# Six weight buffers at six offsets past multiples of 512 bytes, and a smaller scratch for dynamic DMAs

## The chip, the cores and the metric

The kernel runs on one core of one Trainium2 chip. Five engines with queues of their own share the core's SBUF, a memory of 128 partitions: TensorE (PE in the rows; its weight loads stand apart as PEld), VectorE (DVE), ScalarE (ACT), GpSimd (POOL) and SyncE (SP, which issues most DMAs). The metric is device microseconds of one execution. The kernel before takes 622.99 us, the median of 2 runs (622.51 to 623.47).

## The reference

One decoder layer on x of 512 rows and 1024 columns, all in float32:

```python
xn = rms_norm(h, g_mix_norm[l])
proj = xn @ w_in[l]                                  # 1024 x 2560: q, k, v, and u for the convolution
attn = moba_attention(q, k, to_heads(v))             # 8 heads of 64, blocks of 256
conv = conformer_conv(u, b_glu[l], w_dw[l], b_dw[l], g_conv_ln[l], b_conv_ln[l])   # GLU, 31 taps, LayerNorm, swish
h = h + jnp.concatenate([attn, conv], axis=-1) @ w_out[l]
ff = jnp.square(jax.nn.relu(rms_norm(h, g_mlp_norm[l]) @ w_mlp_in[l]))             # 1024 x 4096
h = h + ff @ w_mlp_out[l]                            # 4096 x 1024
return rms_norm(h, g_final)
```

## The kernel before, in words

Every large product is made of float32 values that are split in two: a high part, which is the value rounded to the type fp32r, and a low part, the rest. A product is then three matmuls: high by high, high by low and low by high. `mm3` (L155 to L161) issues the three one after the other into one PSUM bank, on lines L158, L159 and L160. Each of these matmuls loads its own stationary operand first, 128 rows by 128 columns (a LDWEIGHTS in the rows), and then streams a moving operand of 512 or 256 columns past it. A stationary tile is 512 bytes in a partition, a moving one 2048 or 1024.

The weights are cut into 92 units of 128 by 1024 values. For each unit SP loads `raw` (4 buffers), ACT makes the high part `wh` (L115), and DVE, at a few places POOL, makes the low part `wl` (L116). There are three buffers for `wh` and three for `wl`, used in turn: these are the six weight buffers. Four of the units, those of the second half of w_out, go to other buffers (`ffhw`, `fflw`, L126 and L127).

The stages, in order of time:

- u (to about 60 us): the convolution's inputs. The stationary operand is a piece of `wh` or `wl`, the moving one is x, transposed and split (`xh`, `xl`).
- q, k, v, attention and convolution (60 to 227 us): the moving operand of q, k and v is `wh` or `wl`, the stationary one `xh` or `xl`. DVE and POOL run the 31 taps of the convolution here (L300, L323). A table of places (`T`) sets the order of the attention's steps.
- y (200 to 263 us): the output projection, then the second norm and transposes into `hTh`, `hTl`.
- MLP (263 to 611 us): four chunks. In each, `ff` (8 blocks) has the stationary operand in `wh` or `wl` and the moving one in `hTh` or `hTl`; then `z` (two halves) has the moving operand in `wh` or `wl` and the stationary one in `ffh` or `ffl`.
- The last norm and the stores.

Where the buffers lie: in the kernel before all six weight buffers begin at a multiple of 4096 bytes, and so do `xh`, `xl` (later `mixh`, `mixl`), `hTh`, `hTl`, `ffh` and `ffl`. The last four are in the pool `pm`, which takes the place of the attention's pool `pa`; a tile `shift` that nothing uses (L689) sets where `pm` begins. A piece of 128 columns is 512 bytes, so that every stationary and every moving operand of the stages u, q, k, v, y, ff and z begins at a multiple of 512 bytes.

The only DMAs that POOL issues are two on L422, which copy `qs` from one half of the partitions to the other. The scratch for dynamic DMAs is 16 KB at the beginning of SBUF.

Of the kernel before, what the change touches and what calls it, by code (L numbers as in the profile page):

```python
# [10 lines left out]
F32 = mybir.dt.float32  # L11
FR = mybir.dt.float32r
# [5 lines left out]
P = 128  # L18
# [36 lines left out]
def hybrid_layer(ctx: ExitStack, tc: tile.TileContext, x, pack, w_in, w_out, g_mlp, w1, w2, g_fin, out):  # L55
    nc = tc.nc

    perm = ctx.enter_context(tc.tile_pool(name="perm", bufs=1))
# [9 lines left out]
    def f32(ap):  # L68
        return ap.bitcast(F32)
# [23 lines left out]
    raws, parts = {}, {}  # L93
    RAW, SPL = 4, 3

    def load_unit(pieces=1, between=None):
        n = len(raws)
        if n < len(srcs):
            raw = perm.tile([P, 1024], F32, tag="raw", name=f"raw{n}", bufs=RAW)
            a = srcs[n].shape[1]  # L100
            for i in range(pieces):
                r = slice(i * a // pieces, (i + 1) * a // pieces)
                nc.sync.dma_start(raw.rearrange("p (a b) -> p a b", a=a)[:, r], srcs[n][:, r])
                if between and i < pieces - 1:
                    between()
            raws[n] = raw

    def split_unit(pieces=1, low=nc.vector, between=None):
        n = len(parts)
        if n < len(srcs):  # L110
            hi = perm.tile([P, 1024], FR, tag="wh", name=f"wh{n}", bufs=SPL)
            lo = perm.tile([P, 1024], FR, tag="wl", name=f"wl{n}", bufs=SPL)
            for i in range(pieces):
                c = slice(i * 1024 // pieces, (i + 1) * 1024 // pieces)
                nc.scalar.copy(hi[:, c], raws[n][:, c])  # L115
                low.tensor_tensor(lo[:, c], raws[n][:, c], f32(hi[:, c]), op=OP.subtract)  # L116
                if between:
                    between(i)
            a = srcs[n].shape[1]
            parts[n] = (hi.rearrange("p (a b) -> p a b", a=a), lo.rearrange("p (a b) -> p a b", a=a))  # L120
            load_unit()

    def resident_unit(hi, lo):
        n = len(parts)
        raw = raws[n].rearrange("p (a b) -> p a b", a=srcs[n].shape[1])
        nc.scalar.copy(hi, raw)  # L126
        eng(f"er{n % 4}").tensor_tensor(lo, raw, f32(hi), op=OP.subtract)  # L127
        parts[n] = None
        nunit[0] += 1
        load_unit()  # L130
# [3 lines left out]
    def unit(ahead=2):  # L134
        n = nunit[0]
        nunit[0] += 1
        while len(parts) < min(n + 1 + ahead, len(srcs)):
            split_unit()
        return parts[n]
# [39 lines left out]
    nc.sync.dma_start(pk, pack)  # L179
    load_x(1, slice(0, 512))  # L180
    load_unit(2, load_rest)
    load_unit(2)
    load_unit()
# [94 lines left out]
    transpose_half(0, tx)  # L278
    store_half(0, tx, range(0, 4))
    split_unit(4, low=nc.gpsimd, between=lambda i: i and store_half(0, tx, range(2 * i + 2, min(2 * i + 4, KD))))  # L280
    split_unit(4)
    split_unit()
    for t in range(NT):
# [402 lines left out]
    phA.close()  # L686
    pm = ctx.enter_context(tc.tile_pool(name="pm", bufs=1, reuse_waits="tile"))

    pm.tile([P, 928], F32, name="shift")  # L689
    gml = perm.tile([P, D], F32, tag="gbc", name="gmlpbc", bufs=1)  # L690
    nc.scalar.dma_start(gml, bass.AP(tensor=g_mlp.tensor, offset=g_mlp.offset, ap=[[0, P], [1, D]]))

# [207 lines left out]
```

## Time and profile before

| | |
|---|---|
| Median of 2 runs | 622.99 us |
| The profiled execution | 623.05 us, of which the trace spans 621.3 us |
| PE busy | 578.2 us (93% of the span) |
| DVE, ACT, POOL busy | 369.7, 266.1, 162.9 us |
| Mean granted clock of TensorE | 0.968 |
| Mean share of the DMA traffic | 92 GB/s |

A row of a timeline has a start, a duration, the engine, the line, the operation and out<-in. Matmuls overlap in the pipeline, so that the duration of one is longer than what it adds; what a matmul adds is the distance from its start to the next one's, and it is read from two rows and the number of matmuls between them. A row of --lines kind has a count after the x, then busy time, the mean of one in ns, and the idle time before. In rows by windows each engine has its busy time and, in brackets, its number of instructions; then come the granted clock, the DMA share and GB/s.

### The profile page before, as it was taken

How to read it: one execution, taken by the hardware profiler on the slowest of the kernel's cores; microseconds unless marked ns; L12 is line 12 of the kernel's file. 1: busy time of each engine (PE TensorE's matmuls, PEld its weight loads, DVE VectorE, ACT ScalarE, POOL GpSimd, SP SyncE). 2: the span in 40 equal slices, each digit the busy share in tenths (PEclk: the TensorE clock that was granted, in tenths of full speed). 3: DMA queues.
4: the chain of work that ended last, by engine and by line, in shares of the span. 5: the costliest groups of instructions: out<-in, count | busy, mean ns of one | idle time of the engine just before them, and what ended most of it. 6: DMA issues, size and time to landing. Idle time of an engine off the chain costs nothing.

```text
span 621.3 us, 7312 instructions
## 1 busy us (share of the span) xinstructions
PE 578.2 (93%) x2768; PEld 476.7 (77%) x2768; DVE 369.7 (59%) x486; ACT 266.1 (43%) x445; POOL 162.9 (26%) x170
## 2 busy tenths in 40 slices
PE   8998692876999999999999999999999999999995
PEld 7986562765767788898888888888888888888884
DVE  4589999999989766746424454431455343345243
ACT  6864263663768773435321144322234222334233
POOL 2496598492887551100000000000000000000002
PEclk9999987896999999999999999999999999999998
DMA  8632122161111156205233322233232333222203
GB/s 265 153 98 66 38 68 67 35 135 34 56 47 35 35 205 169 69 1 170 101 102 101 93 78 102 102 102 101 72 99 101 103 101 102 86 86 99 69 0 137
DMA packets 59380, 57.22 MB, mean 92 GB/s; under 512 B 1872, under 2 KB 42960, under 8 KB 59344
## 3 DMA queue, kind: packets, MB, share of 16 engines
q1 hardware_dynamic: 58512, 54.64, 28.6%
q0 software_dynamic: 544, 1.05, 1.0%
q10 hardware_dynamic: 288, 1.05, 0.4%
q8 instruction: 22, 0.36, 0.2%
q14 instruction: 14, 0.11, 0.1%
HBM read 53.59 MB, written 2.10 MB: 90 GB/s over the span
## 4 chain that ended last, share of the span: by engine, by line
PE 76%; DVE 15%; issue 3%; ACT 2%; POOL 2%; DMA 1%; SPq 0%; POOLq 0%; ACTq 0%; DVEq 0%
DVE acc L300 10%; PE ff L159 9%; PE ff L158 9%; PE ff L160 9%; PE z L159 9%; PE z L158 9%; PE z L160 9%; DVE wl L116 3%; PE y L158 2%; PE y L160 2%; PE y L159 2%; PE u L160 1%; PE u L159 1%; PE u L158 1%; PE pt L497 1%
## 5 line engine op out<-in xcount | busy, mean ns | idle before, releaser
L116 DVE TENSOR_TENSOR wl<-raw,wh 128x1024 fp32r<-128x1024 f32 (+1 forms) x86 | 113.2, 1318 | 100.6 <-ACT wh L115 100.3
L115 ACT CAST wh<-raw 128x1024 fp32r<-128x1024 f32 (+1 forms) x94 | 92.6, 991 | 117.8 <-PE z L160 75.3
L323 POOL TENSOR_TENSOR acc<-acc,ct 128x512 f32<-128x512 f32 x60 | 98.2, 1636 | 23.2 <-ACT ct L313 19.5
L158 PE MATMUL ff<-hTh,wh 128*128 128x512 f32 (+1 forms) x280 | 103.9, 371 | 0.0
L159 PE MATMUL ff<-hTl,wh 128*128 128x512 f32 (+1 forms) x280 | 103.8, 371 | 0.0
L160 PE MATMUL ff<-hTh,wl 128*128 128x512 f32 (+1 forms) x280 | 103.8, 371 | 0.0
L159 PE MATMUL z<-wl,ffh 128*128 128x512 f32 (+1 forms) x264 | 101.0, 383 | 0.0
L158 PE MATMUL z<-wh,ffh 128*128 128x512 f32 (+1 forms) x264 | 101.0, 383 | 0.0
L160 PE MATMUL z<-wh,ffl 128*128 128x512 f32 (+1 forms) x264 | 101.0, 383 | 0.0
L699 POOL TENSOR_SCALAR ms0f<-ms_f 128x1 f32<-128x1 f32 x4 | 0.8, 192 | 328.7 <-ACT f L223 328.7
L300 DVE SCALAR_TENSOR_TENSOR acc<-hin,pk,acc 128x512 f32<-128x512 f32 x60 | 83.0, 1384 | 1.4
L763 DVE TENSOR_TENSOR sq<-rl 128x512 f32<-128x512 f32 x32 | 22.2, 692 | 64.3 <-ACT rl L761 64.3
L158 PEld LDWEIGHTS ff<-hTh,wh 128*128 128x128 f32 x280 | 52.8, 188 | 9.1
L160 PEld LDWEIGHTS ff<-hTh,wl 128*128 128x128 f32 x280 | 52.7, 188 | 9.0
L159 PEld LDWEIGHTS ff<-hTl,wh 128*128 128x128 f32 x280 | 52.8, 188 | 9.0
L158 PEld LDWEIGHTS z<-wh,ffh 128*128 128x128 f32 x264 | 49.6, 188 | 9.8
L160 PEld LDWEIGHTS z<-wh,ffl 128*128 128x128 f32 x264 | 49.6, 188 | 9.7
L159 PEld LDWEIGHTS z<-wl,ffh 128*128 128x128 f32 x264 | 49.6, 188 | 9.6
L761 ACT ACTIVATE rl<-ff 128x512 f32<-128x512 f32 x32 | 19.2, 599 | 82.6 <-PE ff L160 82.6
L313 ACT ACTIVATE ct<-hin,pk 128x512 f32<-128x512 f32 x60 | 41.5, 719 | 17.9 <-POOL acc L323 17.5
L765 DVE TENSOR_TENSOR ffl<-sq,ffh 128x512 fp32r<-128x512 f32 x32 | 22.2, 693 | 21.9 <-ACT ffh L764 21.9
L764 ACT CAST ffh<-sq 128x512 fp32r<-128x512 f32 x32 | 19.8, 620 | 25.5 <-DVE sq L763 25.5
(162 smaller groups left out, 899.5 us busy)
## 6 DMA issues: line engine op xcount, KB each, us to landing
raw<-w SPq DMA_DIRECT2D x64, 512.0 KB, 3.9
raw<-w_in SPq DMA_DIRECT2D x18, 512.0 KB, 3.7
raw<-w_out SPq DMA_DIRECT2D x8, 512.0 KB, 3.7
xr<-x SPq DMA_DIRECT2D x4, 512.0 KB, 5.0
out<-ot SPq DMA_DIRECT2D x8, 256.0 KB, 2.0
x<-x SPq DMA_DIRECT2D x4, 256.0 KB, 4.4
raw<-w_in SPq DMA_DIRECT2D x4, 256.0 KB, 5.9
x<-x SPq DMA_DIRECT2D x2, 512.0 KB, 6.9
```

Source lines behind the costliest of these rows:

```text
L115: nc.scalar.copy(hi[:, c], raws[n][:, c])
L116: low.tensor_tensor(lo[:, c], raws[n][:, c], f32(hi[:, c]), op=OP.subtract)
L158: nc.tensor.matmul(ps, sh, mh, start=first, stop=False)
L159: nc.tensor.matmul(ps, sh, ml, start=False, stop=False)
L160: nc.tensor.matmul(ps, sl, mh, start=False, stop=last)
L300: nc.vector.scalar_tensor_tensor(accs[i], hins[i][:, j:j + S], wtap(i, j), accs[i], op0=OP.mult, op1=OP.add)
L313: nc.scalar.activation(tmp, hins[i][:, j:j + S], AF.Copy, scale=wtap(i, j))
L323: nc.gpsimd.tensor_tensor(acc, acc, products[n], op=OP.add)
L761: nc.scalar.activation(rl, ps, AF.Relu)
L763: nc.vector.tensor_mul(sq, rl, rl)
L764: nc.scalar.copy(ff["h"][:, b], sq)
L765: nc.vector.tensor_sub(ff["l"][:, b], sq, f32(ff["h"][:, b]))
```

## The change

```diff
+    WH_AT, WL_AT = (16, 64, 8), (96, 32, 48)
...
     def split_unit(pieces=1, low=nc.vector, between=None):
         n = len(parts)
         if n < len(srcs):
-            hi = perm.tile([P, 1024], FR, tag="wh", name=f"wh{n}", bufs=SPL)
-            lo = perm.tile([P, 1024], FR, tag="wl", name=f"wl{n}", bufs=SPL)
+            b = n % SPL
+            hi = perm.tile([P, 1152], FR, tag=f"wh{b}", name=f"wh{n}", bufs=1)[:, WH_AT[b]:WH_AT[b] + 1024]
+            lo = perm.tile([P, 1152], FR, tag=f"wl{b}", name=f"wl{n}", bufs=1)[:, WL_AT[b]:WL_AT[b] + 1024]
...
-    pm.tile([P, 928], F32, name="shift")
+    pm.tile([P, 1184], F32, name="shift")
...
-    nc = bacc.Bacc("TRN2", target_bir_lowering=False, num_devices=1)
+    nc = bacc.Bacc("TRN2", target_bir_lowering=False, num_devices=1, dynamic_dma_scratch_size=8192)
```

Each weight buffer grows by 512 bytes, and the 1024 values begin at a different place in it: past a multiple of 512 bytes, the three `wh` begin at 0x40, 0x100 and 0x20, the three `wl` at 0x180, 0x80 and 0xC0. The scratch for dynamic DMAs falls from 16 KB to 8 KB, which makes the room. Tiles ahead of the weight buffers move down by 8192 bytes, those of `pa` by 5120, and those of `pm`, with the longer `shift`, by 4096: `xh`, `xl`, `hTh`, `hTl`, `ffh` and `ffl` still begin at multiples of 4096 bytes.

Nothing else changes. The built program has the same 4521 instructions in the same order on every engine, and every wait is for the same semaphore at the same value. What differs is the start of an operand in the weight buffers, in 2280 matmuls, in the 94 instructions that write a `wh` and in the 94 that read it and write a `wl` (the first two units are split in four pieces).

## Rows read from the trace of the kernel before

**Rows 1.** Page, part 1: busy time by engine.
```profile
PE 578.2 (93%) x2768; PEld 476.7 (77%) x2768; DVE 369.7 (59%) x486; ACT 266.1 (43%) x445; POOL 162.9 (26%) x170
```
**Rows 2.** Page, part 4: the chain that ended last, by engine, by line.
```profile
PE 76%; DVE 15%; issue 3%; ACT 2%; POOL 2%; DMA 1%; SPq 0%; POOLq 0%; ACTq 0%; DVEq 0%
DVE acc L300 10%; PE ff L159 9%; PE ff L158 9%; PE ff L160 9%; PE z L159 9%; PE z L158 9%; PE z L160 9%; DVE wl L116 3%; PE y L158 2%; PE y L160 2%; PE y L159 2%; PE u L160 1%; PE u L159 1%; PE u L158 1%; PE pt L497 1%
```
**Rows 3.** Busy time by windows: the convolution and attention, then the MLP.
```profile
60.00:227.00 167.00, 136.60 (x636) 104.52 (x634) 152.66 (x236) 102.70 (x201) 115.17 (x98) 0.90 0.22 67
263.00:611.00 348.00, 348.00 (x1622) 291.71 (x1621) 147.40 (x168) 107.82 (x145) 3.41 (x11) 1.00 0.29 90
```
**Rows 4.** Timeline of PE in z, first and last of 16 matmuls.
```profile
400.01 0.39 PE L160 MATMUL z<-wh,ffl 128*128 128x512 f32 x1
...
403.41 0.39 PE L160 MATMUL z<-wh,ffl 128*128 128x512 f32 x1
```
**Rows 5.** Timeline of PE in ff, first and last of 16 matmuls.
```profile
285.09 0.39 PE L160 MATMUL ff<-hTh,wl 128*128 128x512 f32 x1
...
288.49 0.39 PE L160 MATMUL ff<-hTh,wl 128*128 128x512 f32 x1
```
**Rows 6.** Timeline of PE in ff with 256 columns, first and last of 19.
```profile
264.03 0.28 PE L160 MATMUL ff<-hTh,wl 128*128 128x256 f32 x1
...
266.19 0.28 PE L160 MATMUL ff<-hTh,wl 128*128 128x256 f32 x1
```
**Rows 7.** Timeline of PE in q, first and last of six matmuls.
```profile
60.88 0.63 PE L160 MATMUL q<-wh,xl 128*128 128x512 f32 x1
...
63.01 0.47 PE L159 MATMUL q<-wl,xh 128*128 128x512 f32 x1
```
**Rows 8.** Windows around rows 7 and rows 4: the granted clock is third from last.
```profile
60.00:63.00 3.00, 3.00 (x8) 2.32 (x7) 2.93 (x3) 2.78 (x4) 2.84 (x3) 0.50 0.63 180
400.00:403.40 3.40, 3.40 (x16) 2.81 (x15) 0.88 (x1) 1.05 (x1) 0.00 (x0) 1.00 0.43 157
```
**Rows 9.** By line and shape: matmuls with an operand in a weight buffer.
```profile
L158 PE MATMUL z<-wh,ffh 128*128 128x512 f32 x248 | 96.5, 389 | 0.0
L158 PE MATMUL ff<-hTh,wh 128*128 128x512 f32 x232 | 90.3, 389 | 0.0
L158 PE MATMUL u<-xh,wh 128*128 128x512 f32 x40 | 15.6, 389 | 0.0
L158 PE MATMUL u<-xh,wh 128*128 128x256 f32 x48 | 13.8, 288 | 0.0
L158 PE MATMUL ff<-hTh,wh 128*128 128x256 f32 x48 | 13.7, 284 | 0.0
L158 PE MATMUL z<-wh,ffh 128*128 128x256 f32 x16 | 4.5, 281 | 0.0
```
**Rows 10.** Timeline of PE after a break: q (ten matmuls), then z (six).
```profile
63.32 0.39 PE L160 MATMUL q<-wh,xl 128*128 128x512 f32 x1
...
65.41 0.39 PE L160 MATMUL q<-wh,xl 128*128 128x512 f32 x1
...
594.07 0.40 PE L158 MATMUL z<-wh,ffh 128*128 128x512 f32 x1
...
595.23 0.39 PE L160 MATMUL z<-wh,ffl 128*128 128x512 f32 x1
```
**Rows 11.** By line and shape: the low parts on DVE, 60:227, then 263:611.
```profile
L116 DVE TENSOR_TENSOR wl<-raw,wh 128x1024 fp32r<-128x1024 f32 x11 | 21.4, 1941 | 0.8 <-ACT wh L115 0.7
L116 DVE TENSOR_TENSOR wl<-raw,wh 128x1024 fp32r<-128x1024 f32 x61 | 74.8, 1226 | 93.4 <-ACT wh L115 93.4
```
**Rows 12.** DMAs that POOL issues, and the first matmul that needs them.
```profile
123.84 1.49 POOL L422 DMA_DIRECT2D qs<-qs  x2 [1.60 <-ACT qs L416]
DMA to landing us min/median/max: 6.0/6.7/7.4
L467 PEld LDWEIGHTS s<-ks,qs x32: 186/190/195, 153.1 to 217.5; 128*128 128x128 f32 x32
```

## The prediction

> **What bounds the kernel now.** I read the busy times first: PE is busy 93% of the span, the next engine 59% [rows 1]. The chain of waits says the same with an order in it: 76% of the time up to the end runs over PE, the three passes of ff and z alone take 54%, and DVE has 15%, mostly the convolution's taps [rows 2]. Windows by stage then show that these are two different kernels in one. In the convolution and attention PE is busy 136.6 of 167 us and DVE 152.7; in the MLP PE is busy in every one of 348 us and DVE in 147 [rows 3]. So the MLP costs what its matmuls cost, and a change of each matmul by one nanosecond shows there in full.
>
> What does one matmul cost? In z, 15 steps from one start to the next take 3.40 us, 226.7 ns each [rows 4]. In ff, where the weight buffer is the stationary operand and no longer the moving one, 15 steps also take 3.40 us [rows 5]. [...]
>
> **The change part by part.** No instruction, order or wait changes, so there is nothing to remove or add; all of it is addresses. [...] How many matmuls have an operand in a weight buffer? In z and ff 248 + 232 of 512 columns and 16 + 48 of 256, each in three passes: 1632. In u 40 + 48, three times: 264 [rows 9]. Together 1896. (q, k, v and the first half of y have more, but lie mostly where PE has idle time.) One nanosecond for each is 1.9 us, of which 1.63 us in z and ff, where PE never idles.
>
> The trace has no row for a weight buffer at another offset: stationary and moving operands of these stages all begin at multiples of 512 bytes. [...] Nearer rows: after a break PE does not step at 226.7 at once. Nine steps of q at the full clock take 2.09 us, 232 ns each, and five steps of z just after matmuls of 256 columns take 1.16 us, also 232 [rows 10]. [...] I take zero, because ff and z, with the weight buffer in opposite roles and opposite activations beside it, agree to the tenth of a nanosecond, as a cost that belongs to the pair of instructions would, whatever their addresses.
>
> [...]
>
> ACT and DVE now write the parts at other offsets. In the MLP one low part takes 1226 ns on DVE, and DVE waits 93.4 us for ACT around them [rows 11]: covered, since DVE is busy 147 of 348 us, and a tenth more (7.5 us over the 61) stays covered. In the convolution there are 11 on DVE with a mean of 1941 ns, and DVE sets the pace there. Their offsets are as equal as those of the 61, so what makes them longer is not the offset. As bounds, all 11 at 1226 ns would be 7.9 us less, and as much again longer 7.9 us more; I take zero.
>
> The scratch: POOL issues its two copies at 123.84 us, they land 6.0 and 7.4 us after their issue, and the first matmul that reads `qs` loads at 153.1 [rows 12]. The slack is about 21 us. If half the room made the second issue wait until the first copy has landed, POOL's next taps would be up to 7.4 us late. That is the upper bound, although POOL has only 2% of the chain [rows 2]; the other end is nothing, since a smaller scratch takes no work away. I take zero.
>
> The sum is zero against the profiled execution, 623.05 us with a span of 621.3, which stands within 0.1 us of the median. I predict **623.0 us**.
>
> **The rivals.**
>
> Faster: weight load and moving read get in each other's way because both begin at the same place past 512 bytes, and the offsets part them. [...] Against it: in the matmul the two reads run through 512 and 2048 bytes, so different beginnings still pass the same places. [...]
>
> Slower: equal offsets are what lets the three passes settle at 226.7. With six different ones each matmul's two reads stand differently to each other than those of the matmul before, PE stays in the unsettled spacing after a break [rows 10], and pays 5.3 ns more for each: 10.1 us, 633.1. From 6.6 ns a matmul on (12.5 us) it is over 2%; at 240 ns it would be 648. For it: the spacing was off just after a change in the pattern. Against it: ff and z change buffers for every unit and don't leave 226.7.
>
> Elsewhere: DVE's low parts in the convolution or POOL's second copy move, by up to 7.9 us either way: 615 to 631.
>
> **How the numbers follow.** Forecast, spacing within 2 ns of 226.7: 0.53, from 619 to 627. Faster rival: 0.25, of which 0.16 beyond 2% (below 610.5, half the excess and more) and 0.09 with only some of the six buffers gaining. Slower rival: 0.17, of which 0.09 beyond 2% (above 635.5). Elsewhere: 0.05, within 2%. Two per cent, 12.5 us, is about what a measurement of this kernel can tell from no change for sure. So faster 0.16, same 0.75, slower 0.09. The range goes from 606, which leaves out the cases in which most of the excess goes (about 0.10), to 634, which takes in the unsettled spacing and leaves out the rest of the slower rival (about 0.10).
>
> **What would show it.** In the changed kernel's timeline 15 steps of z and of ff should again take 3.40 us; 3.30 or less means the faster rival, and then ff and z should both show it; 3.48 means the slower one. If only some buffers matter, the step changes with the unit, every third one alike. Windows should leave the MLP at 348 us with PE always busy, DVE's 61 low parts at 1226 ns, its 11 at about 1.9 us, and POOL's copies landing before 153 us. The forecast is wrong if the MLP's stretch moves by more than 4 us while instructions and waits are the same.

## The result, and the profile after

The changed kernel takes 630.28 us (629.77 to 630.79, 2 runs), 1.0117 times the kernel before, with a 95% interval from 1.0068 to 1.0166. It is slower, by 7.3 us, less than 2%. Its profiled execution spans 629.1 us, 7.8 more than before. The lines of the changed kernel stand 3 further down (L158 is L161, L116 is L119).

Page of the changed kernel, part 1, and then windows as in [rows 3]:

```profile
PE 587.5 (93%) x2768; PEld 478.3 (76%) x2768; DVE 369.9 (59%) x486; ACT 265.9 (42%) x445; POOL 163.5 (26%) x170
```
```profile
60.00:227.00 167.00, 136.48 (x632) 103.79 (x633) 153.16 (x237) 103.29 (x202) 116.17 (x98) 0.90 0.22 67
263.00:611.00 348.00, 348.00 (x1590) 286.22 (x1589) 145.20 (x164) 105.81 (x141) 1.77 (x7) 1.00 0.29 88
```

PE is busy 9.3 us longer, DVE, ACT and POOL by less than 0.7. PE never idles in the MLP, as before, but in the same 348 us it starts 1590 matmuls and not 1622. The MLP's length settles where the time went. These are its first and its last matmul, of the kernel before and of the changed one:

```profile
263.08 0.28 PE L158 MATMUL ff<-hTh,wh 128*128 128x256 f32 x1
...
613.35 0.28 PE L160 MATMUL z<-wh,ffl 128*128 128x256 f32 x1
```
```profile
263.78 0.28 PE L161 MATMUL ff<-hTh,wh 128*128 128x256 f32 x1
...
621.27 0.28 PE L163 MATMUL z<-wh,ffl 128*128 128x256 f32 x1
```

350.27 us have become 357.49: 7.2 of the 7.8 us. Now the steps. The timeline of PE in the changed kernel shows here the first matmul of each of four units of ff, then of five of z; a unit is 24 matmuls.

```profile
354.10 0.39 PE L161 MATMUL ff<-hTh,wh 128*128 128x512 f32 x1
...
359.69 0.39 PE L161 MATMUL ff<-hTh,wh 128*128 128x512 f32 x1
...
365.25 0.39 PE L161 MATMUL ff<-hTh,wh 128*128 128x512 f32 x1
...
370.81 0.39 PE L161 MATMUL ff<-hTh,wh 128*128 128x512 f32 x1
...
398.68 0.39 PE L161 MATMUL z<-wh,ffh 128*128 128x512 f32 x1
...
404.18 0.40 PE L161 MATMUL z<-wh,ffh 128*128 128x512 f32 x1
...
409.78 0.39 PE L161 MATMUL z<-wh,ffh 128*128 128x512 f32 x1
...
415.33 0.39 PE L161 MATMUL z<-wh,ffh 128*128 128x512 f32 x1
...
420.92 0.39 PE L161 MATMUL z<-wh,ffh 128*128 128x512 f32 x1
```

Three units of ff take 16.71 us, 232.1 ns a matmul, where [rows 5] had 226.7. By unit they take 5.59, 5.56 and 5.56 us; before it was 24 x 226.7 = 5.44. In z the units take 5.50 us (buffers at 0x100 and 0x80), 5.60 (0x20 and 0xC0) and 5.55 (0x40 and 0x180): the step hangs on the buffer, but not on it alone. The fourth of these units has the same two buffers as the first and takes 5.59 us, 232.9 ns a step for 229.2; the seven other whole z units with these buffers take as long, so that the first is the exception. Over all of ff and z the 512-column steps, averaged from the records, went from 226.76 to 231.93 ns. 1440 of them by 5.17 ns are 7.4 us; the 192 with 256 columns are a little shorter than before (119.0 against 120.1 ns), which gives 0.2 us back. The sum, 7.2 us, is the MLP's whole difference.

At the low clock nothing changed. In q of the changed kernel six steps, with buffers at 0x40 and 0x180, take 2.56 us, 426.7 ns each, and [rows 7] had 426; the window's granted clock (third from last) is 0.50:

```profile
69.66 0.63 PE L163 MATMUL q<-wh,xl 128*128 128x512 f32 x1
...
72.22 0.51 PE L163 MATMUL q<-wh,xl 128*128 128x512 f32 x1
```
```profile
69.66:72.20 2.54, 2.54 (x7) 1.98 (x6) 2.50 (x2) 0.00 (x0) 2.09 (x2) 0.50 0.65 204
```

In every run of this document the steps of q, k and v with 512 columns at this clock, where PE doesn't wait, are 426 to 428 ns in the records, whatever the offsets.

The low parts on DVE, 60:227 and then 263:611, answer to [rows 11], and POOL's copies with their first reader to [rows 12]:

```profile
L119 DVE TENSOR_TENSOR wl<-raw,wh 128x1024 fp32r<-128x1024 f32 x12 | 22.0, 1830 | 0.9 <-ACT wh L118 0.9
L119 DVE TENSOR_TENSOR wl<-raw,wh 128x1024 fp32r<-128x1024 f32 x61 | 74.7, 1225 | 96.1 <-ACT wh L118 96.1
```
```profile
DMA to landing us min/median/max: 4.5/5.3/6.2
L470 PEld LDWEIGHTS s<-ks,qs x32: 186/190/195, 153.5 to 217.9; 128*128 128x128 f32 x32
```

DVE takes 1225 ns, and 1226 before; the copies land no later after their issue. Neither the writes at other offsets nor the smaller scratch shows a cost here.

### The profile page after: what moved, and what is told of

Same layout as the page of the kernel before. It is cut to its first block, busy times and chain, and to the rows that moved or that the text cites. A ratio compares the mean times of both kernels' runs of the same rounds, so it can differ in the third digit from the quotient of the medians.

```text
span 629.1 us, 7312 instructions
## 1 busy us (share of the span) xinstructions
PE 587.5 (93%) x2768; PEld 478.3 (76%) x2768; DVE 369.9 (59%) x486; ACT 265.9 (42%) x445; POOL 163.5 (26%) x170
## 4 chain that ended last, share of the span: by engine, by line
PE 75%; DVE 16%; issue 3%; POOL 3%; ACT 2%; DMA 1%; SPq 0%; POOLq 0%; ACTq 0%; DVEq 0%
PE ff L162 9%; PE ff L163 9%; PE ff L161 9%; DVE acc L303 9%; PE z L161 9%; PE z L163 9%; PE z L162 9%; DVE wl L119 3%; PE y L161 2%; PE y L163 2%; PE y L162 2%; POOL acc L326 2%; PE u L161 1%; PE u L162 1%; PE u L163 1%
## 5 line engine op out<-in xcount | busy, mean ns | idle before, releaser
L119 DVE TENSOR_TENSOR wl<-raw,wh 128x1024 fp32r<-128x1024 f32 (+1 forms) x86 | 112.5, 1311 | 103.6 <-ACT wh L118 103.5
L163 PE MATMUL ff<-hTh,wl 128*128 128x512 f32 (+1 forms) x280 | 105.2, 376 | 0.0
L162 PE MATMUL ff<-hTl,wh 128*128 128x512 f32 (+1 forms) x280 | 105.1, 375 | 0.0
L161 PE MATMUL ff<-hTh,wh 128*128 128x512 f32 (+1 forms) x280 | 105.0, 375 | 0.0
L161 PE MATMUL z<-wh,ffh 128*128 128x512 f32 (+1 forms) x264 | 102.4, 388 | 0.0
L161 PEld LDWEIGHTS ff<-hTh,wh 128*128 128x128 f32 x280 | 53.0, 189 | 10.2
L161 PEld LDWEIGHTS z<-wh,ffh 128*128 128x128 f32 x264 | 49.5, 188 | 11.0
```

Source lines behind the costliest of these rows:

```text
L161: nc.tensor.matmul(ps, sh, mh, start=first, stop=False)
L162: nc.tensor.matmul(ps, sh, ml, start=False, stop=False)
L163: nc.tensor.matmul(ps, sl, mh, start=False, stop=last)
```

## The experiments

Each edit is shown against the changed kernel. All but e1 and e11 ran once; their verdicts rest on steps, and on the MLP's length, which was 350.27 us in the kernel before and the same to the hundredth in the three variants below that undo the effect. Whole times of the kernel before went from 622.0 to 626.4 us in the runs beside them, so that a single time says less than its MLP.

**e1_zero.** The scratch and the moved pools alone.

```diff
-    WH_AT, WL_AT = (16, 64, 8), (96, 32, 48)
+    WH_AT, WL_AT = (0, 0, 0), (0, 0, 0)
```

Expected: 

> The changed kernel with all six buffers back at multiples of 512 bytes, the larger tiles and the 8 KB scratch kept. If the offsets made it slower: steps of 226.7 ns in ff and z and 623 us. If the scratch or the moved pools did: about 630 us and an MLP that is longer than before.

Measured: 623.25 us, ratio to the kernel before 1.0003 (0.9985 to 1.0021). Three units of ff, from the timeline of PE, first matmul of the first and of the fourth:

```profile
351.88 0.39 PE L161 MATMUL ff<-hTh,wh 128*128 128x512 f32 x1
...
368.20 0.39 PE L161 MATMUL ff<-hTh,wh 128*128 128x512 f32 x1
```

72 steps take 16.32 us, 226.7 ns each. This kernel differs from the changed one in the offsets alone, so the offsets are the cause.

**e2_same_a, e3_same_b, e4_same_c.** Are unequal offsets the trouble, or each offset by itself? Within a buffer number wh and wl now begin at one offset (table entries count values of 4 bytes).

```diff
-    WH_AT, WL_AT = (16, 64, 8), (96, 32, 48)
+    WH_AT, WL_AT = (8, 16, 24), (8, 16, 24)         # e2_same_a
+    WH_AT, WL_AT = (32, 48, 64), (32, 48, 64)       # e3_same_b
+    WH_AT, WL_AT = (80, 96, 112), (80, 96, 112)     # e4_same_c
```

Expected of e2: 

> Within a buffer number, wh and wl begin at the same offset: 0x20, 0x40, 0x60 for the three. Theory 'unequal offsets' (what costs is that a matmul's operand begins at another offset than the one before it): in each unit of ff the three passes now have equal stationary offsets, so ff settles at 226.7 ns and about 623 to 625 us come out, since only a change of unit disturbs it. Theory 'distance to the activations' (each offset against the activations' 0 has a price of its own): ff and z keep 229 to 236 ns and differ by buffer, some 628 to 633 us.

Expected of e3: 

> As the one before with 0x80, 0xC0, 0x100. 'Unequal offsets': ff at 226.7 ns in every buffer, 623 to 625 us. 'Distance to the activations': a price for each of the three offsets, 228 to 236 ns.

Expected of e4: 

> As the two before with 0x140, 0x180, 0x1C0. 'Unequal offsets': ff at 226.7 ns, 623 to 625 us. 'Distance to the activations': a price for each, and if some offset is better than 0, steps below 226 ns show here or in the two before.

Measured: 634.73, 629.74 and 629.37 us, one run each. e2 lies above the 633 that was expected at most: its MLP is 8.2 us longer than before, and it begins 3.3 us later, which is not explained. The units of ff in e3, with offsets 0x100, 0x80 and 0xC0 in this order:

```profile
354.53 0.40 PE L161 MATMUL ff<-hTh,wh 128*128 128x512 f32 x1
...
360.00 0.40 PE L161 MATMUL ff<-hTh,wh 128*128 128x512 f32 x1
...
365.58 0.39 PE L161 MATMUL ff<-hTh,wh 128*128 128x512 f32 x1
...
371.08 0.39 PE L161 MATMUL ff<-hTh,wh 128*128 128x512 f32 x1
```

5.47, 5.58 and 5.50 us: 228, 232.5 and 229 ns. "Unequal offsets" falls: with equal ones 0x80 still costs. Only 0x100 is nearly as good as 0: in its unit the first three steps are 236, 233 and 231 ns and the last one, in which the next unit's weights are loaded, 232; the twenty between are 226 or 227. The buffers that have 0xC0 in e3 have 0x40 in e2; here they are, first as the stationary operand in ff, then as the moving one in z:

```profile
368.00 0.40 PE L161 MATMUL ff<-hTh,wh 128*128 128x512 f32 x1
...
373.60 0.39 PE L161 MATMUL ff<-hTh,wh 128*128 128x512 f32 x1
...
418.32 0.40 PE L161 MATMUL z<-wh,ffh 128*128 128x512 f32 x1
...
423.82 0.40 PE L161 MATMUL z<-wh,ffh 128*128 128x512 f32 x1
```

5.60 us, 233.3 ns, against 5.50, 229.2: the same offset has another price in the other role. In ff it is 0xC0 (e3 above, 229) that costs what 0x40 costs in z.

**e7_mix256.** The counter-test: unequal offsets, but 256 bytes apart.

```diff
-    WH_AT, WL_AT = (16, 64, 8), (96, 32, 48)
+    WH_AT, WL_AT = (0, 64, 0), (64, 0, 64)
```

Expected: 

> The six buffers alternate between offsets 0 and 0x100, so that every pass and every unit has another offset than the one before. Theory 'distance' with a period of 256 bytes: all of them count as 0, 226.7 to 227.5 ns and 623 to 625 us. Theory 'unequal offsets': 229 ns and more, 628 us or more.

Measured: 623.67 us beside 624.02 for the kernel before, and an MLP of 350.27 us.

```profile
352.58 0.39 PE L161 MATMUL ff<-hTh,wh 128*128 128x512 f32 x1
...
368.90 0.39 PE L161 MATMUL ff<-hTh,wh 128*128 128x512 f32 x1
```

16.32 us for 72 steps, 226.7 ns each: no cost. So in these runs only what lies past multiples of 256 bytes counts of the two operands' places: 0x100 beside 0 costs 226.7 ns as 0 does, and 0x140 in z costs 229.3 ns (e4) where 0x40 costs 229.4.

**e6_shift_all** and **e12_acts.** Is it the weight buffers' own alignment, or their distance to the activations? e6 moves both by 128 bytes; e12 leaves the weights at 0 and moves the MLP's activations.

```diff
-    WH_AT, WL_AT = (16, 64, 8), (96, 32, 48)
+    WH_AT, WL_AT = (0, 0, 0), (0, 0, 0)
...
+    perm.tile([P, 32], F32, name="pad")             # e6_shift_all alone: ahead of xh
...
-    pm.tile([P, 1184], F32, name="shift")
+    pm.tile([P, 1216], F32, name="shift")           # e12_acts alone
```

Expected of e6: 

> Weight buffers and all activations of these stages begin 128 bytes past multiples of 512: no distance between them, none at a multiple of 256. Theory 'distance': 226.7 ns and about 623 us. Rival 'alignment' (an operand that does not begin at a multiple of 256 bytes costs more by itself): 232 to 233 ns as with 0x80 alone, about 632 us.

Expected of e12: 

> The weight buffers stay at multiples of 512 bytes and the tiles of the MLP (hTh, hTl, ffh, ffl) begin 128 bytes past them, by a longer unused tile ahead of them. Theory 'distance': ff and z as with the weight buffers at 0x80, 232 to 233 ns, while u stays at 226.7; the MLP some 359 us, the whole 631 to 632 us. If it were the offset of what is written by ACT and DVE, or of the weight buffers as such, the MLP stays at 350 us and the whole at 623.

Measured for e6: 625.93 us in one run, an MLP of 350.27 us; its 2.9 us more span lie ahead of the MLP, where steps are as before, and are unexplained but within what the kernel before shows between runs. Three units of ff:

```profile
354.86 0.39 PE L161 MATMUL ff<-hTh,wh 128*128 128x512 f32 x1
...
371.18 0.39 PE L161 MATMUL ff<-hTh,wh 128*128 128x512 f32 x1
```

Measured for e12: 631.37 us and an MLP of 358.17 us; u stays at 226.9 ns.

```profile
353.91 0.39 PE L161 MATMUL ff<-hTh,wh 128*128 128x512 f32 x1
...
370.64 0.39 PE L161 MATMUL ff<-hTh,wh 128*128 128x512 f32 x1
```

16.32 us for e6 (226.7 ns), 16.73 for e12 (232.4 ns). In the built program of e6 every operand of u, y, ff and z begins 128 bytes past a multiple of 256, and nothing is lost; in e12 the weight buffers begin at multiples of 512 as in the kernel before, and the loss is back. In these runs the distance between the moving and the stationary operand decides, whoever was moved.

**e5_fine** and **e9_more.** Is there a distance better than 0?

```diff
-    WH_AT, WL_AT = (16, 64, 8), (96, 32, 48)
+    WH_AT, WL_AT = (2, 4, 12), (2, 4, 12)           # e5_fine
+    WH_AT, WL_AT = (1, 20, 28), (1, 20, 28)         # e9_more
```

Expected of e5: 

> Offsets below the grid used so far: 8, 16 and 48 bytes, equal for wh and wl of a buffer. Theory 'distance' (the price of a matmul hangs on where the moving operand begins against the stationary one, past multiples of 256 bytes; on the 32-byte grid 0 costs 226.7 ns, +64 costs 229.3, the others 232 to 234): a price for each; if the price grows from 0 on smoothly, 8 bytes is between 226.7 and 230 and 16 near 230. If only whole pieces of 32 or 64 bytes count, 8 and 16 stay at 226.7. A step under 226 ns at one of them would point to a faster kernel.

Expected of e9: 

> Offsets 4, 80 and 112 bytes, equal for wh and wl of a buffer, so that with both roles the distances 4, 252, 80, 176, 112 and 144 past multiples of 256 are seen. From the distances looked at so far (0: 226.7 ns, 64: 229.3, the others 231 to 234) each of these should cost 229 to 235 ns with 512 columns and the MLP 354 us or more; a distance with less than 226 would point to a faster kernel.

Measured: 631.91 and 632.56 us. One unit of z in e9, with the buffers at 4 bytes:

```profile
343.47 0.40 PE L161 MATMUL z<-wh,ffh 128*128 128x512 f32 x1
...
349.14 0.40 PE L161 MATMUL z<-wh,ffh 128*128 128x512 f32 x1
```

5.67 us, 236 ns a step, more than the 235 that was expected at most. With one offset for wh and wl, a buffer at offset d stands at distance +d in z, where it moves, and at -d in ff, where it is stationary. From all runs of that kind, mean step with 512 columns, worked out from the starts in the records:

```
start of the moving operand less that of the stationary one, modulo 256 bytes: ns a step
  0: 226.7 (kernel before, e1, e6, e7)
 +4: 236.6     -4: 232.4
 +8: 233.7     -8: 230.9
+16: 231.7    -16: 233.4
+32: 233.2    -32: 233.2
+48: 231.6    -48: 233.3     (+48: five units at 229.8 to 230.0, five at 233.0 to 233.4)
+64: 229.4    -64: 233.3     (again with 0x140: 229.3, 233.2; with 0xC0 and 0x1C0: 229.3 to 229.4, 233.1 to 233.3)
+80: 231.2    -80: 231.9
+96: 233.8    -96: 233.7
+112: 231.2   -112: 233.4
 128: 232.3 to 233.0
```

Where one distance was seen in ff and in z (0, +64, -64 and 128), it gives the same step within 0.7 ns: 0x40 in z and 0xC0 and 0x1C0 in ff are one distance and cost 229.3 to 229.4. There is no slope towards 0, as e5 had thought possible; four bytes already cost up to 10 ns, and no mean of this table is below 226.7. But a distance does not always fix the step. At +48 the ten whole units of z fall in two groups, 3 ns apart, as the units with 0x100 and 0x80 do in the changed kernel. Which of the two rhythms a unit takes may hang on what ran before it; that was not tested.

**e8_low_only** and **e10_high_only.** Which passes pay?

```diff
-    WH_AT, WL_AT = (16, 64, 8), (96, 32, 48)
+    WH_AT, WL_AT = (0, 0, 0), (32, 32, 32)          # e8_low_only
+    WH_AT, WL_AT = (32, 32, 32), (0, 0, 0)          # e10_high_only
```

Expected of e8: 

> Only the three wl begin at 0x80, the three wh at 0. If each pass pays by its own two operands, only the one pass of three with wl pays (about 233 ns), the other two stay at 226.7: 625 us. If what counts is the moving operand against the weights that are loaded meanwhile, which are those of the next pass, then in ff the pass on line 162 pays, in z again the one with wl. If a pass leaves something to the next, more than one pass pays: about 628 us.

Expected of e10: 

> The three wh begin at 0x80, the three wl at 0. Reading of the run with wl alone: a matmul pays when its moving operand lies at a distance from its own weights or from those that are loaded while it runs. Then in ff all three passes pay (the first by both, the second by its own, the third by the next), 231 ns or more each, and in z the first and third, with the moving wh, while the second stays near 227. If only the weights loaded meanwhile count, the second pass of ff stays at 226.7; if only its own, the third. About 630 us.

Measured: 628.92 and 628.21 us. In e8, three units of ff, then two of z:

```profile
353.69 0.39 PE L161 MATMUL ff<-hTh,wh 128*128 128x512 f32 x1
...
370.33 0.39 PE L161 MATMUL ff<-hTh,wh 128*128 128x512 f32 x1
...
398.06 0.39 PE L161 MATMUL z<-wh,ffh 128*128 128x512 f32 x1
...
409.05 0.39 PE L161 MATMUL z<-wh,ffh 128*128 128x512 f32 x1
```

231.1 ns in ff and 229.0 in z: the same buffers cost about twice as much where they are stationary. By pass, again from the starts in the records (the step from the start of a matmul to the next start is put down to the first of the two):

```
ns a step          first pass   second pass   third pass
e8  ff             226.7        232.5         234.2        (third: own weights wl; second: wl is loaded for the third)
e8  z              227.0        233.8         226.4        (second: wl moves)
e10 ff             232.7        232.3         234.8
e10 z              232.3        226.0         228.4        (first and third: wh moves)
```

So in ff of e8 two matmuls pay for one displaced stationary tile: the one it belongs to (234.2 ns), and the one before it (232.5), during which its load stands in the trace. Here is such a matmul of e8, the second pass, with the load for the third:

```profile
356.69 0.40 PE L162 MATMUL ff<-hTl,wh 128*128 128x512 f32 x1
356.69 0.19 PEld L163 LDWEIGHTS ff<-hTh,wl 128*128 128x128 f32 x1
```

e10's forecast held in ff: all three passes pay, since wh belongs to two of them and is loaded during the third and the first. In z the first pass pays 5.6 ns and the third only 1.7, for which there is no explanation. In z of e8 a displaced moving tile makes its own matmul pay alone, 233.8 ns beside 227.0 and 226.4. Why a distance has a price was not shown: the rows have the starts of loads and matmuls, and nothing of what happens inside them.

**e11_best.** Distance 0 everywhere, but 64 bytes for the six units whose matmuls all have 256 columns, which took 116 ns there (e2, the units of ff with 0x40).

```diff
-    WH_AT, WL_AT = (16, 64, 8), (96, 32, 48)
...
-            b = n % SPL
-            hi = perm.tile([P, 1152], FR, tag=f"wh{b}", name=f"wh{n}", bufs=1)[:, WH_AT[b]:WH_AT[b] + 1024]
-            lo = perm.tile([P, 1152], FR, tag=f"wl{b}", name=f"wl{n}", bufs=1)[:, WL_AT[b]:WL_AT[b] + 1024]
+            b, at = n % SPL, 16 if n in (0, 1, 2, 28, 29, 30) else 0
+            hi = perm.tile([P, 1152], FR, tag=f"wh{b}", name=f"wh{n}", bufs=1)[:, at:at + 1024]
+            lo = perm.tile([P, 1152], FR, tag=f"wl{b}", name=f"wl{n}", bufs=1)[:, at:at + 1024]
```

Expected: 

> Distance 0 for all units but six (0 to 2 and 28 to 30), whose matmuls all have 256 columns and begin at 64 bytes, where 256 columns took 116 ns and not 120. 288 matmuls by 4 ns: 1.2 us less than the kernel before at most, 622 us or a ratio of 0.998; in the MLP 0.6 us less than its 350.3. If it is lost in waits of the first stages, no difference.

Measured: 623.23 us, ratio 0.9993 (0.9974 to 1.0011), 12 runs. First and last matmul of its MLP:

```profile
262.26 0.28 PE L159 MATMUL ff<-hTh,wh 128*128 128x256 f32 x1
...
612.05 0.28 PE L161 MATMUL z<-wh,ffl 128*128 128x256 f32 x1
```

The MLP takes 349.79 us, 0.48 less than before, as 144 steps of 117.1 ns for 120.4 should give. The whole shows no difference that can be told: a gain of this size is below the spread of the runs.

## Why the prediction was right in its range and wrong in its cause

630.28 us lies in the range, and a change within 2% had most of the chance. But the forecast itself, 623.0 with 619 to 627 around it, rested on a step that failed, and by its own sign it was wrong: the MLP moved by 7.2 us, more than 4, with the same instructions and waits. The range held by luck as far as the forecast goes: it reached up to 634 only to take in the slower rival. Point by point:

- **What bounds the kernel** held: the MLP is as long as its matmuls, and 7.2 of 7.8 us show there.
- **The price of an offset** was taken as zero, because ff and z agreed to the tenth of a nanosecond with the weight buffer in opposite roles. That is the step that failed. Both stages had the same distance, 0, so their agreement said nothing about another one. The measured price in the MLP is 5.2 ns for a matmul of 512 columns and about -1.1 ns for one of 256; in z of e9 four bytes of distance took the step from 226.7 to 236.6 ns. The prediction had the better witness in its own rows: the same buffers at 232 ns after a break [rows 10], which it used only to price a rival.
- **The faster rival** had the sign wrong: for 512 columns distance 0, with 226.7 ns, is the best found and not the collision. Its chances and the lower end of the range are counted in an excess, time of a step that its columns don't need; that was the author's estimate, and no run shows such a part of a step: with 512 columns no distance has a mean step below 226.7 ns at a granted clock of 1.00. At 0.50 the steps were 426 to 428 ns, at distance 0 and at the others.
- **The slower rival** had 0.17 and the right size for a step: 5.3 ns, measured 5.2; 15 steps at 231.9 ns are its 3.48 us. Its time, 633.1, was too long mainly because it charged the matmuls of 256 columns as well. Its reason, that unequal offsets keep PE unsettled, fell in e2 to e4 and e7; its argument against itself was the same error as above.
- **ACT and DVE, the scratch, the order** at zero: all three held, shown by e1 and the rows above.

The rows after a break say more than the prediction took from them. Those of q in [rows 10] end at 65.41 us; the kernel before goes on like this:

```profile
65.64 0.39 PE L158 MATMUL q<-wh,xh 128*128 128x512 f32 x1
...
66.32 0.39 PE L158 MATMUL q<-wh,xh 128*128 128x512 f32 x1
```

Three steps take 0.68 us, 226.7 ns each: at distance 0 PE settles after some ten matmuls of 224 to 236 ns. At other distances steps of that kind go on to the end of the unit: in the changed kernel's z they repeat 227, 234, 226 from 398.68 us on, and 230, 236, 234 from 415.33 us on. So the slower rival had nearly the right state, a PE that doesn't settle at 226.7, and the wrong condition for it.

Left open: why a step at distance 0 is 226.7 ns at a granted clock of 1.00 and not about 213, an estimate that halves the 426 ns at 0.50 [rows 7, rows 8]; what makes 64 (229.4 ns) better than its neighbours 48 and 80 (231.6 and 231.2); and what chooses between two rhythms at one distance.

## What to carry to other kernels

In this stream of fp32r matmuls that each load weights, at a granted clock of 1.00, where the two operands begin relative to each other was worth 1 to 4% of a step (226.7 ns at distance 0, 229.3 to 236.6 at the others). With 512 columns the best place found for the moving and the stationary buffers was the same one past multiples of 256 bytes, an MLP of 350.27 us against 357.49 in the changed kernel: try it first, and keep it so when a tile ahead of them grows. Two stages that agree don't show that a parameter is without effect if the parameter is the same in both: ask which rows differ in it. And a price seen anywhere for the same instructions with the same buffers, here 232 ns after a break, can be a better first guess for the price of a disturbance than zero.

## What the runs showed of the hardware that was not expected

In these runs the mean step of an fp32r matmul with its weight load hung on the operands' distance (the moving one's start less the stationary one's) modulo 256 bytes: 226.7 ns at 0, 229.3 to 229.4 at 64, 230.9 to 236.6 at the other distances tried, with 512 columns at a granted clock of 1.00. Four bytes of distance cost 9.9 ns in z and 5.7 in ff (e9). At 48 bytes the units of z had two lasting rhythms, 229.8 to 230.0 ns in five and 233.0 to 233.4 in five (e5). With 256 columns the order was another: 120 ns at 0, and 116 to 118 in the units of ff at a distance of 64 or 192 (e2, e3, e4). A displaced weight tile slowed two matmuls, its own to 234.2 ns and the one before to 232.5 (e8, ff), and a displaced moving tile one, to 233.8 (e8, z). At the granted clock of 0.50 none of it is seen, with 426 to 428 ns a step in every run.
